# Transposes of values and keys by VectorE in 32x32 blocks, placed by GpSimd, in a bidirectional RWKV-7 and short-convolution step

## The chip, the core and the metric

The kernel runs on one core of a Trainium2 chip. The metric is the device time of one execution in microseconds (us). Five engines work side by side, each through its own instructions in order: PE (TensorE, matmuls; its weight loads are listed apart as PEld), DVE (VectorE), ACT (ScalarE), POOL (GpSimd) and SP (SyncE, which here only issues DMAs).

## What is computed

One layer of a diffusion backbone for 128 context tokens and 256 latent tokens, 2048 channels. After a norm, one projection `h @ w_in` feeds an RWKV-7 time mixing in both directions and a gated short convolution; both go through output projections, are merged by gates and projected again. All is float32. The part that the change touches is the time mixing, whose recurrence for each of 32 heads of 64 channels is

```python
sa = einsum('dbhij,dbhj->dbhi', S, a_t)
S = S * w_t[..., None, :] + sa[..., :, None] * b_t[..., None, :] + v_t[..., :, None] * k_t[..., None, :]
y = einsum('dbhij,dbhj->dbhi', S, r_t)
```

in two directions `d`, from a zero state for the context and from a given state for the latent tokens. `w` is the decay, `k` the key, `v` the value, `a = -kk` and `b = kk * a`.

## The kernel before

**Blocks.** The recurrence is done for 16 blocks of two heads (`b`, 128 channels on the partitions), each in chunks of 64 tokens: six chunks for each direction, twelve in all (`f`). Within a chunk the recurrence becomes matrices. The stages of one block, each a generator:

- `prep_a`, `prep_k`: decay, learning rate and normalised key of the next block, by small matmuls and elementwise work.
- `prep_b` (line 664): `pr` (queries times decay) and `bk` (keys over decay) are multiplied on PE to the decay products `pA` (line 700), twelve matmuls of two passes each for a direction; VectorE masks them into the tile `A` (line 706). A triangular 32x32 system in each half chunk has then to be inverted: its blocks go by DMA through DRAM (`ui`, line 710) into a tile `U` of 48 partitions (line 716), 60 small dependent VectorE instructions solve it in place (lines 721 and 723; called *the solve* below), ScalarE makes the transposed copy `UT` (line 727), and both go back by DMA through DRAM (`uo`, lines 728 and 729) into `A` (line 734) and a tile `x11` (line 735; the profile calls it `x`). GpSimd multiplies `bk` by the chunk's last decay in between (line 713).
- `prep_c` (line 737): PE transposes the values into `pv` (six transposes of 128x128, line 761; ScalarE copies the values reversed in time first, for the second direction, line 758), and ten of the twelve chunks of `bk` into `pb` (line 770); ScalarE copies these out of PSUM into `sav` and `bt` (lines 763 and 771). Then come the products `pav` (line 776), whose result goes behind the values into `sav`, and a GpSimd memset of the lower half of `A` (line 783).
- `scan` (line 794): first the corner products `pH` from `x11` and `A` (line 852) and `pX`; then two chains of chunks, context and latent, each step `po`, `pq`, `pu`, and last `py` (line 893), which reads `sav`.
- `norm` (line 910) and `finish` (line 927): a group norm on VectorE with a power on GpSimd (`rs`, line 924), then three PE transposes of the result (`py` again, line 931).

**What fills PE.** Beside this runs the stream of the large projections (`Stream`): all weights are loaded in raw tiles of 1 MB (two buffers), split by ScalarE and VectorE into a high and a low part (`whi`, line 88, and `wlo`, line 89, three buffers each), and each product is three matmuls (lines 81 to 83, called a *triple* below) into `d_...` tiles. PE's order is written out by hand: every `yield n` of a stage puts `n` triples behind it, `prep_b` yields PB0 = 14 and PB1 = 6 (line 93), and before `scan` the triples are filled up to WINDOW = 80 (line 974; 104 in the first block, 96 in the last). So each steady block has the same number of triples, 160, whatever the yields within `prep_c` are. The other engines' orders, SP's too, are made by a scheduler from dependencies, priorities and its own estimate of times; their instructions wait in that order.

Of the kernel before, what the change touches and what calls it, by code (L numbers as in the profile page):

```python
# [56 lines left out]
def hybrid_step(ctx, tc, cst, x_prompt, x_sample, state_f, state_b, c, c_ctx, ada_w, ada_b, norm_g,  # L57
# [605 lines left out]

    def prep_b(b, o):

        r, kk = r_[b], o["kk"]
# [27 lines left out]
        for d in range(2):  # L694
            pr, bk = o["pr"][d], o["bk"][d]
            m0 = C_MB if d else C_MF
            pas = {(h, n0): bank(f"pA_{b}_{d}_{h}_{n0}") for n0 in (0, 4) for h in range(2)}
            for n in range(NCH):
                for h in range(2):
                    TE.matmul(pas[h, n // 4 * 4][:, n % 4, :], bk[hss[h], n, :], pr[hss[h], n, :],  # L700
                              start=True, stop=True)
            for n0, w in ((0, 4), (4, 2)):
                mk = cs[:, m0:m0 + P].rearrange("p (w t) -> p w t", t=C).unsqueeze(1).broadcast_to([P, w, 2, C])
                for h in range(2):
                    f0 = NCH * d + n0
                    V.tensor_tensor(A[:, :, f0:f0 + w, hss[h]].rearrange("p w n t -> p n w t"),
                                    pas[h, n0][:, 0:w, :].rearrange("p n (w t) -> p n w t", t=C), mk, ALU.mult)
# [4 lines left out]
        for d in range(2):
            G.tensor_tensor(o["bk"][d][:], o["bk"][d][:], o["ep"][d][:, :, C:C + 1].broadcast_to([P, NCH, P]), ALU.mult)
# [13 lines left out]
        S.copy(UT[:], U[:].rearrange("p a b -> p b a"))  # L727
# [8 lines left out]

    def prep_c(b, o):

        r, v, A = r_[b], v_[b], o["A"]
# [10 lines left out]
        sav = sp.tile([P, 2 * NCH, P], F32, tag="sav", name=f"sav_{b}")  # L750
        bt = sp.tile([P, 2 * NCH, P], F32, tag="bt", name=f"bt_{b}")
        o["sav"], o["bkt"] = sav, bt
        for d in range(2):
            if d == 0:
                src = v
            else:
                src = tmp(f"vr_{b}")
                S.copy(src[:], v[:, ::-1])
            pv = bank(f"pv_{b}_{d}")
            for q in range(3):  # L760
                TE.transpose(pv[:, q, :], src[:, q * P:(q + 1) * P], ident)
# [405 lines left out]
```

## Time and profile before

| what | value |
|---|---|
| time, median of 3 runs | 2238.22 us (2237.42 to 2239.56) |
| the profiled execution's own time | 2242.0 us |
| its span, first to last instruction | 2240.2 us |
| PE busy, its weight loads | 97%, 92% |
| DVE, ACT, POOL busy | 69%, 47%, 5% |
| DMA | 339.97 MB, mean 152 GB/s |
| granted TensorE clock | 0.996 |

Busy shares are of the span. In a timeline a row gives the start in us from the span's start, the duration in us, the engine, the line, the operation, out<-in and shapes, and in brackets the idle time before it and what ended it. PE's durations overlap, since matmuls are pipelined: what one costs is read from the distance between starts.

### The profile page before, as it was taken

The numbers are of one execution on the slowest core, as the hardware profiler recorded it, in microseconds if no ns is written. First come the engines' busy times: TensorE is split into PE (matmuls) and PEld (weight loads), VectorE is DVE, ScalarE is ACT, GpSimd is POOL, SyncE is SP. The second block draws the span as 40 slices with busy tenths as digits, with TensorE's granted clock in tenths as the row PEclk, the third lists the DMA queues.
The fourth block names the chain that finished last, engine by engine and source line by source line (L and its number), as shares of the span: only waits on it lengthen the run. The fifth ranks groups of instructions, "written<-read, shape, count | busy, mean of one in ns | idle before, by whom it ended". The sixth has DMA issues, their size and how long they took to land.

```text
span 2240.2 us, 40545 instructions
## 1 busy us (share of the span) xinstructions
PE 2179.2 (97%) x16020; PEld 2064.9 (92%) x16020; DVE 1540.2 (69%) x3208; ACT 1044.3 (47%) x1800; POOL 116.5 (5%) x113
## 2 busy tenths in 40 slices
PE   5899999999999999999999999999999999999998
PEld 3588999999999999999999999999999999998988
DVE  3248567787777778777878787777777774444354
ACT  4245445454545454454545454546455543333333
POOL 2000010101010100000010101010100000000000
PEclk9999999999999999999999999999999999999999
DMA  9973544444444445443444434444445455886633
GB/s 335 346 211 116 147 129 133 111 120 125 112 125 120 113 117 132 115 132 103 124 109 133 111 110 134 112 118 140 120 121 143 146 179 162 292 281 230 221 132 113
DMA packets 440397, 339.97 MB, mean 152 GB/s; under 512 B 95552, under 2 KB 421776, under 8 KB 439312
## 3 DMA queue, kind: packets, MB, share of 16 engines
q1 hardware_dynamic: 438720, 335.63, 51.1%
q8 instruction: 126, 2.06, 0.4%
q10 hardware_dynamic: 432, 1.57, 0.2%
q14 instruction: 63, 0.52, 0.1%
q0 software_dynamic: 1056, 0.19, 0.1%
HBM read 307.37 MB, written 29.36 MB: 150 GB/s over the span
## 4 chain that ended last, share of the span: by engine, by line
PE 81%; DVE 8%; DMA 5%; ACT 3%; SPq 2%; issue 1%; POOL 0%; POOLq 0%; ACTq 0%; DVEq 0%
PE d_rk L81 4%; PE d_rk L83 4%; PE d_rk L82 4%; PE d_gv L81 3%; PE d_gv L82 3%; PE d_gv L83 3%; DMA raw_adah<-in_ada_w_dram 3%; PE pA L700 2%; PE d_oa L81 2%; PE d_oa L83 2%; PE d_oa L82 2%; PE d_bc L81 2%; PE d_mb L81 2%; PE d_bc L83 2%; PE d_bc L82 2%; PE d_bx L81 2%
## 5 line engine op out<-in xcount | busy, mean ns | idle before, releaser
L721 DVE TENSOR_TENSOR ut<-U 48x30 f32<-48x30 f32 (+14 forms) x480 | 154.6, 322 | 16.2 <-DMA U<-ui 4.1
L81 PE MATMUL d_rk<-h_hi,whi_rk 128*128 128x384 f32 x480 | 163.0, 340 | 0.6 <-ACT lst L554 0.6
L723 DVE TENSOR_TENSOR U<-U,ut 48x30 f32<-48x30 f32 (+14 forms) x480 | 154.5, 322 | 12.1
L81 PE MATMUL d_gv<-h_hi,whi_gv 128*128 128x384 f32 x480 | 161.0, 335 | 0.0
L83 PE MATMUL d_gv<-h_hi,wlo_gv 128*128 128x384 f32 x480 | 160.7, 335 | 0.0
L82 PE MATMUL d_gv<-h_lo,whi_gv 128*128 128x384 f32 x480 | 160.7, 335 | 0.0
L83 PE MATMUL d_rk<-h_hi,wlo_rk 128*128 128x384 f32 x480 | 160.4, 334 | 0.0
L82 PE MATMUL d_rk<-h_lo,whi_rk 128*128 128x384 f32 x480 | 160.4, 334 | 0.0
L88 ACT CAST whi_gv<-raw_gv 128x1024 fp32r<-128x1024 f32 (+1 forms) x64 | 64.0, 1000 | 139.6 <-PE d_rk L82 96.9
L88 ACT CAST whi_rk<-raw_rk 128x1024 fp32r<-128x1024 f32 x60 | 63.0, 1054 | 106.4 <-PE d_rk L82 31.7
L89 DVE TENSOR_TENSOR wlo_rk<-raw_rk,whi_rk 128x1024 fp32r<-128x1024 f32 x60 | 72.9, 1218 | 44.9 <-ACT whi_rk L88 39.7
L81 PE MATMUL d_gb<-h_hi,whi_gb 128*128 128x384 f32 x256 | 92.2, 360 | 0.0
L924 POOL TENSOR_TENSOR rs<-var,nhalf 128x6 f32<-128x6 f32 x16 | 21.2, 1325 | 1364.1 <-DVE var L922 1364.1
L81 PE MATMUL d_bc<-h_hi,whi_bc 128*128 128x384 f32 x256 | 92.2, 360 | 0.0
L81 PE MATMUL d_bg<-h_hi,whi_bg 128*128 128x384 f32 x256 | 92.1, 360 | 0.0
L81 PE MATMUL d_bx<-h_hi,whi_bx 128*128 128x384 f32 x256 | 92.1, 360 | 0.0
L81 PEld LDWEIGHTS d_rk<-h_hi,whi_rk 128*128 128x128 f32 x480 | 90.1, 188 | 1.8 <-ACT lst L554 0.9
L81 PE MATMUL d_ma<-h_hi,whi_ma 128*128 128x384 f32 x256 | 91.7, 358 | 0.0
L81 PE MATMUL d_ob<-ybh,whi_ob 128*128 128x384 f32 x256 | 88.9, 347 | 2.6 <-ACT whi_ob L88 2.1
L81 PEld LDWEIGHTS d_gv<-h_hi,whi_gv 128*128 128x128 f32 x480 | 90.5, 189 | 0.2
L82 PEld LDWEIGHTS d_gv<-h_lo,whi_gv 128*128 128x128 f32 x480 | 90.5, 188 | 0.0
L83 PEld LDWEIGHTS d_gv<-h_hi,wlo_gv 128*128 128x128 f32 x480 | 90.4, 188 | 0.0
(315 smaller groups left out, 6641.9 us busy)
## 6 DMA issues: line engine op xcount, KB each, us to landing
raw_adah<-in_ada_w_dram SPq DMA_DIRECT2D x64, 512.0 KB, 8.6
raw_rk<-in_w_in_dram SPq DMA_DIRECT2D x60, 512.0 KB, 5.3
raw_gv<-in_w_in_dram SPq DMA_DIRECT2D x60, 512.0 KB, 4.9
raw_ma<-in_w_in_dram SPq DMA_DIRECT2D x16, 1024.0 KB, 5.5
raw_mb<-in_w_in_dram SPq DMA_DIRECT2D x16, 1024.0 KB, 5.7
raw_bc<-in_w_in_dram SPq DMA_DIRECT2D x16, 1024.0 KB, 5.5
raw_bx<-in_w_in_dram SPq DMA_DIRECT2D x16, 1024.0 KB, 5.4
raw_bg<-in_w_in_dram SPq DMA_DIRECT2D x16, 1024.0 KB, 5.5
```

The lines of the kernel that those rows point to most:

```text
L81: TE.matmul(out, wh, xh, start=start, stop=False)
L82: TE.matmul(out, wh, xl, start=False, stop=False)
L83: TE.matmul(out, wl, xh, start=False, stop=stop)
L88: S.copy(hi[0:rows], src)
L89: V.tensor_tensor(lo[0:rows], src, hi[0:rows].bitcast(F32), ALU.subtract)
L700: TE.matmul(pas[h, n // 4 * 4][:, n % 4, :], bk[hss[h], n, :], pr[hss[h], n, :], start=True, stop=True)
L721: V.tensor_tensor(tv, U[:, 0:s, s:s + 1].broadcast_to([48, s, w]), U[:, s:s + 1, s + 1:].broadcast_to([48, s, w]), ALU.mult)
L723: V.tensor_tensor(U[:, 0:s, s + 1:], U[:, 0:s, s + 1:], tv, ALU.add)
L924: G.tensor_tensor(rs[:], var[:], nhalf[:], ALU.pow)
```

## The change

The sixteen PE transposes of a block go, and with them the PSUM tiles `pv` and `pb`, six `yield 1` of `prep_c` and ten ScalarE copies (one reversed copy of the values, four out of `pv`, four out of `pb`, and that of `UT`). In their place:

- at the start of `prep_b` VectorE transposes the values of a direction in 32x32 blocks into a temporary `vt` (two instructions of 128x384), and GpSimd copies the blocks where they belong in `sav`: 16 copies of 32 partitions x 192 elements;
- behind the last mask of `A`, VectorE transposes `bk` in place in 32x32 blocks (two instructions of 128x768), and GpSimd copies the blocks into `bt`, all twelve chunks: 32 copies of the same size;
- the transposed copy `UT` is GpSimd's.

```diff
     def prep_b(b, o):
-        r, kk = r_[b], o["kk"]
+        r, kk, v = r_[b], o["kk"], v_[b]
+        sav = sp.tile([P, 2 * NCH, P], F32, tag="sav", name=f"sav_{b}")
+        o["sav"] = sav
+        for d in range(2):
+            x = tmp(f"vt_{b}_{d}")
+            V.transpose(x[:], v[:, ::-1] if d else v[:])
+            x = x[:].rearrange("p (n e t) -> p n e t", e=2, t=32)
+            for e in range(2):
+                for q in range(4):
+                    G.tensor_copy(sav[C + 32 * e:C + 32 * e + 32, NCH * d:NCH * d + NCH, 32 * q:32 * q + 32],
+                                  x[32 * q:32 * q + 32, :, e, :])
...
         for d in range(2):
-            G.tensor_tensor(o["bk"][d][:], o["bk"][d][:], o["ep"][d][:, :, C:C + 1].broadcast_to([P, NCH, P]), ALU.mult)
+            o["lam"] = G.tensor_tensor(o["bk"][d][:], o["bk"][d][:], o["ep"][d][:, :, C:C + 1].broadcast_to([P, NCH, P]),
+                                       ALU.mult).ins
+        with tc.issue_after(last):
+            for d in range(2):
+                V.transpose(flat(o["bk"][d][:]), flat(o["bk"][d][:]))
...
-        S.copy(UT[:], U[:].rearrange("p a b -> p b a"))
+        G.tensor_copy(UT[:], U[:].rearrange("p a b -> p b a"))
...
     def prep_c(b, o):
-        for d in range(2):
-            if d == 0:
-                src = v
-            else:
-                src = tmp(f"vr_{b}")
-                S.copy(src[:], v[:, ::-1])
-            pv = bank(f"pv_{b}_{d}")
-            for q in range(3):
-                TE.transpose(pv[:, q, :], src[:, q * P:(q + 1) * P], ident)
-            for e in range(2):
-                S.copy(sav[C:P, NCH * d + e:NCH * d + NCH:2, :], pv[C * e:C * e + C, 0:3, :])
-            yield 1
-        for d in range(2):
-            for n0, n1 in (((0, 4), (4, 5)), ((0, 3), (4, 6)))[d]:
-                pb = bank(f"pb_{b}_{d}_{n0}")
-                for n in range(n0, n1):
-                    TE.transpose(pb[:, n - n0, :], o["bk"][d][:, n, :], ident)
-                S.copy(bt[:, NCH * d + n0:NCH * d + n1, :], pb[:, 0:n1 - n0, :])
-                yield 1
+        with tc.issue_after(o["lam"]):
+            for d, p, q in ((d, p, q) for d in range(2) for p in range(4) for q in range(4)):
+                G.tensor_copy(bt[32 * p:32 * p + 32, NCH * d:NCH * d + NCH, 32 * q:32 * q + 32],
+                              o["bk"][d][32 * q:32 * q + 32, :, 32 * p:32 * p + 32])
```

`last` is the last mask of `A`; `issue_after` holds an instruction's place in the order behind the named one. On PE the six triples that stood between the transposes now stand behind `pav`, before the next matmuls of `prep_a`; nothing else moves there. In three places the other engines' orders are of interest. Line numbers behind the change are those of the changed kernel.

GpSimd, from one block's memset of `A` over the end of that block (power `rs`) to the next block's memset, blocks 3 and 4, before:

```order
L783 MEMSET A_5063 64x1536
L924 TENSOR_TENSOR rs_6146<-var_6143,nhalf 128x6
L713 TENSOR_TENSOR bk_0_6150<-bk_0_6150,ep_1148 128x768
L713 TENSOR_TENSOR bk_1_6156<-bk_1_6156,ep_1150 128x768
L783 MEMSET A_6214 64x1536
```

and with the change (`vt_0` and `vt_1` are the two directions' turned values of block 4, `xN` tells of N such instructions):

```order
L782 MEMSET A_5150 64x1536
L743 COPY UT_5310<-U_5246 48x1024
L676 COPY sav_6237<-vt_0_6238 32x6x32 x7
L923 TENSOR_TENSOR rs_6234<-var_6231,nhalf 128x6
L676 COPY sav_6237<-vt_0_6238 32x6x32
L676 COPY sav_6237<-vt_1_6248 32x6x32 x8
L725 TENSOR_TENSOR bk_0_6259<-bk_0_6259,ep_1148 128x768
L725 TENSOR_TENSOR bk_1_6265<-bk_1_6265,ep_1150 128x768
L770 COPY bt_6503<-bk_0_6259 32x6x32 x16
L770 COPY bt_6503<-bk_1_6265 32x6x32 x16
L782 MEMSET A_6323 64x1536
```

The power `rs` of block 3's norm now stands behind seven copies of block 4's values (in 12 of 15 such places; behind 14 in two and 9 in one), and the memset behind the 32 copies of the keys.

VectorE, the end of the solve of block 4, before (`ut` and `U` are the solve, `wlo_bc_0_1` a low part of the stream's weights, `ga` a gate):

```order
L89 TENSOR_TENSOR wlo_bc_0_0_6692<-raw_bc_0_6689,whi_bc_0_0_6691 128x1024
L721 TENSOR_TENSOR ut_6310<-U_6308 48x108
L723 TENSOR_TENSOR U_6308<-U_6308,ut_6310 48x27x4
L721 TENSOR_TENSOR ut_6310<-U_6308 48x84
L725 TENSOR_SCALAR U_6308<-U_6308 48x32
L723 TENSOR_TENSOR U_6308<-U_6308,ut_6310 48x28x3
L721 TENSOR_TENSOR ut_6310<-U_6308 48x58
L723 TENSOR_TENSOR U_6308<-U_6308,ut_6310 48x29x2
L721 TENSOR_TENSOR ut_6310<-U_6308 48x30
L723 TENSOR_TENSOR U_6308<-U_6308,ut_6310 48x30
L89 TENSOR_TENSOR wlo_bc_0_1_6696<-raw_bc_0_6689,whi_bc_0_1_6695 128x1024
L440 TENSOR_TENSOR ga_6735<-ga_6735,d_gv_0_6628 128x384
```

and with the change:

```order
L741 TENSOR_SCALAR U_6419<-U_6419 48x32
L89 TENSOR_TENSOR wlo_bc_0_1_6806<-raw_bc_0_6799,whi_bc_0_1_6805 128x1024
L739 TENSOR_TENSOR U_6419<-U_6419,ut_6421 48x28x3
L737 TENSOR_TENSOR ut_6421<-U_6419 48x58
L739 TENSOR_TENSOR U_6419<-U_6419,ut_6421 48x29x2
L440 TENSOR_TENSOR ga_6845<-ga_6845,d_gv_0_6738 128x384
L737 TENSOR_TENSOR ut_6421<-U_6419 48x30
L739 TENSOR_TENSOR U_6419<-U_6419,ut_6421 48x30
L89 TENSOR_TENSOR wlo_bc_1_0_6887<-raw_bc_1_6884,whi_bc_1_0_6886 128x1024
```

One `wlo` and one `ga` now stand inside the solve. This is so in the even blocks 2 to 12 (in 4, 8 and 12 another `wlo` has moved out ahead of the solve); in the odd ones from 3 on and in 14 the solve holds the same other instructions as before.

SP, the way back of the inverse in block 4, before:

```order
L101 DMA raw_bc_1_6774<-in_w_in_dram 128x8x256
L728 DMA uo_6213<-U_6308 48x1024
L729 DMA uo_6213<-UT_6372 48x1024
L734 DMA A_6214<-uo_6213 32x12x32 x2
L735 DMA x_4_6376<-uo_6213 32x12x32
L734 DMA A_6214<-uo_6213 32x12x32 x2
L735 DMA x_4_6376<-uo_6213 32x12x32
L101 DMA raw_bx_0_6906<-in_w_in_dram 128x8x256
```

and with the change:

```order
L101 DMA raw_bc_1_6884<-in_w_in_dram 128x8x256
L101 DMA raw_bx_0_7016<-in_w_in_dram 128x8x256
L744 DMA uo_6322<-U_6419 48x1024
L745 DMA uo_6322<-UT_6483 48x1024
L621 DMA lraw_0_8049<-in_w_dram 96x2x128
L750 DMA A_6323<-uo_6322 32x12x32 x2
L751 DMA x_4_6487<-uo_6322 32x12x32
L750 DMA A_6323<-uo_6322 32x12x32 x2
L751 DMA x_4_6487<-uo_6322 32x12x32
L101 DMA raw_bx_1_7172<-in_w_in_dram 128x8x256
```

A load of 1 MB of weights now stands ahead of the inverse's way back, and a small load within it, again in the even blocks 2 to 12. In the odd blocks 3 to 13 and in block 14 a 1 MB load stands between `uo<-UT` and `A<-uo` in both kernels.

More of the change, by code (lines that the diff above doesn't have):

```diff
@@ L705, in prep_b @@
                     f0 = NCH * d + n0
-                    V.tensor_tensor(A[:, :, f0:f0 + w, hss[h]].rearrange("p w n t -> p n w t"),
-                                    pas[h, n0][:, 0:w, :].rearrange("p n (w t) -> p n w t", t=C), mk, ALU.mult)
+                    last = V.tensor_tensor(A[:, :, f0:f0 + w, hss[h]].rearrange("p w n t -> p n w t"),
+                                           pas[h, n0][:, 0:w, :].rearrange("p n (w t) -> p n w t", t=C), mk,
+                                           ALU.mult).ins
             yield PB1
@@ L712, in prep_b @@
         for d in range(2):
-            G.tensor_tensor(o["bk"][d][:], o["bk"][d][:], o["ep"][d][:, :, C:C + 1].broadcast_to([P, NCH, P]), ALU.mult)
+            o["lam"] = G.tensor_tensor(o["bk"][d][:], o["bk"][d][:], o["ep"][d][:, :, C:C + 1].broadcast_to([P, NCH, P]),
+                                       ALU.mult).ins
+        with tc.issue_after(last):
+            for d in range(2):
+                V.transpose(flat(o["bk"][d][:]), flat(o["bk"][d][:]))
         U = sp.tile([48, 32, 32], F32, tag="U", name=f"U_{b}")
@@ L737, in prep_c @@
     def prep_c(b, o):
-        r, v, A = r_[b], v_[b], o["A"]
+        r, A, sav = r_[b], o["A"], o["sav"]
         s_in = sp.tile([P, 2, C], F32, tag="s_in", name=f"s_in_{b}")
@@ L748, in prep_c @@
                                       [:, :, 32 * jb:32 * jb + 32])
-        sav = sp.tile([P, 2 * NCH, P], F32, tag="sav", name=f"sav_{b}")
         bt = sp.tile([P, 2 * NCH, P], F32, tag="bt", name=f"bt_{b}")
-        o["sav"], o["bkt"] = sav, bt
-        for d in range(2):
-            if d == 0:
-                src = v
-            else:
-                src = tmp(f"vr_{b}")
-                S.copy(src[:], v[:, ::-1])
-            pv = bank(f"pv_{b}_{d}")
-            for q in range(3):
-                TE.transpose(pv[:, q, :], src[:, q * P:(q + 1) * P], ident)
-            for e in range(2):
-                S.copy(sav[C:P, NCH * d + e:NCH * d + NCH:2, :], pv[C * e:C * e + C, 0:3, :])
-            yield 1
-        for d in range(2):
-            for n0, n1 in (((0, 4), (4, 5)), ((0, 3), (4, 6)))[d]:
-                pb = bank(f"pb_{b}_{d}_{n0}")
-                for n in range(n0, n1):
-                    TE.transpose(pb[:, n - n0, :], o["bk"][d][:, n, :], ident)
-                S.copy(bt[:, NCH * d + n0:NCH * d + n1, :], pb[:, 0:n1 - n0, :])
-                yield 1
+        o["bkt"] = bt
+        with tc.issue_after(o["lam"]):
+            for d, p, q in ((d, p, q) for d in range(2) for p in range(4) for q in range(4)):
+                G.tensor_copy(bt[32 * p:32 * p + 32, NCH * d:NCH * d + NCH, 32 * q:32 * q + 32],
+                              o["bk"][d][32 * q:32 * q + 32, :, 32 * p:32 * p + 32])
         pvs = [bank(f"pav_{b}_{d}") for d in range(2)]
```

## The prediction

> **What bounds the kernel now.** First the page, its span and the engines' shares; then for whom PE waited (us in total, times, longest).
>
> ```profile
> span 2240.2 us, 40545 instructions
> PE 2179.2 (97%) x16020; PEld 2064.9 (92%) x16020; DVE 1540.2 (69%) x3208; ACT 1044.3 (47%) x1800; POOL 116.5 (5%) x113
> ```
>
> ```profile
> PE pada L292 <- DMA raw_adah<-in_ada_w_dram: 22.9, 14, 10.1
> ...
> PE pH L852 <- DMA x<-uo: 0.2, 1, 0.2
> ...
> PE py L931 <- DVE ytok L925: 0.2, 1, 0.2
> ```
>
> PE is busy nearly throughout, and behind the start (`pada`) it waits for almost nobody. What PE no longer does is won, as long as nobody else becomes late. The two waits of 0.2 us tell where that is near: at `pH`, whose operand comes back by DMA from the solve, and at the last `py`, which needs the norm. So I looked at two blocks in the timeline. Block 4 (628 to 733 us): the loads of `x11` with first and last start and time to landing, and the start of `pH`.
>
> ```profile
> L735 SPq DMA_DIRECT2D x<-uo x2: 303/385/467, 679.6 to 681.0; - x2
> ...
> DMA to landing us min/median/max: 1.8/1.9/2.0
> ```
>
> ```profile
> 686.17 0.62 PE L852 MATMUL pH<-x,A 32*32 32x32 f32 x48
> ```
>
> The second load lands at 681.0 + 2.0 = 683.0 at the latest, 3.2 us ahead of `pH`. Block 5 (733 to 838 us), where a 1 MB load of weights stands on SP just ahead of these loads:
>
> ```profile
> L735 SPq DMA_DIRECT2D x<-uo x2: 450/754/1057, 784.8 to 787.2; - x2
> ...
> DMA to landing us min/median/max: 3.7/4.5/5.4
> ```
>
> ```profile
> 791.31 0.62 PE L852 MATMUL pH<-x,A 32*32 32x32 f32 x48
> ```
>
> Here they land at 784.8 + 5.4 = 790.2 and 787.2 + 3.7 = 790.9, 0.4 us ahead of `pH`. What makes this chain long is the solve. VectorE's costliest groups during block 5's solve (749.4 to 778.7 us):
>
> ```profile
> L723 DVE TENSOR_TENSOR U<-U,ut 48x30 f32<-48x30 f32 (+14 forms) x30 | 9.7, 323 | 0.8
> L721 DVE TENSOR_TENSOR ut<-U 48x30 f32<-48x30 f32 (+14 forms) x30 | 9.7, 322 | 1.0 <-DMA U<-ui 0.3
> L89 DVE TENSOR_TENSOR wlo_gv<-raw_gv,whi_gv 128x1024 fp32r<-128x1024 f32 x4 | 4.9, 1213 | 0.0
> ```
>
> VectorE idles 1.8 us in 29: whatever is added to it there, or holds it up there, ends the solve later.
>
> **PE's part.** Block 5's transposes, from the last triple ahead of them to `pav`:
>
> ```profile
> 742.48 0.34 PE L83 MATMUL d_bg<-h_hi,wlo_bg 128*128 128x384 f32 x1
> 742.65 0.49 PE L761 MATMUL pv<-cs,v 128*128 128x128 f32 x3
> 742.89 0.42 PE L81 MATMUL d_bg<-h_hi,whi_bg 128*128 128x384 f32 x1
> 743.15 0.34 PE L82 MATMUL d_bg<-h_lo,whi_bg 128*128 128x384 f32 x1
> ...
> 747.38 0.34 PE L83 MATMUL d_rk<-h_hi,wlo_rk 128*128 128x384 f32 x1
> 747.65 1.61 PE L776 MATMUL pav<-sav,A 64*64 64x64 f32 x48
> ```
>
> Three transposes take 0.24 us, and the first matmul behind them 0.26 where others take 0.17. From 742.65 to 747.65 are 5.00 us. Six triples, at 18 x 0.173, are 3.12 of them, and 0.10 is the step to `pav` (0.27 for 0.17), which stays. That leaves 1.78 us a block, **28.5 us** in 16 blocks. All of it lies between `pA` and `pH`, so PE comes to `pH` 1.78 us earlier against a chain that starts at `pA` as before: at 684.4 in block 4, at 789.5 in block 5. Ten ScalarE copies go too; with ScalarE busy 47% and off this path they count nothing.
>
> **VectorE's part.** Two group rows:
>
> ```profile
> L673 DVE TENSOR_TENSOR bk<-kd,sig 128x384 f32<-128x384 f32 x32 | 17.6, 551 | 0.1
> ...
> L792 DVE STREAM_TRANSPOSE st<-s_in 64x64 f32<-64x64 f32 x64 | 12.2, 221 | 0.6
> ```
>
> A block transpose of 64 columns takes 0.22 us, and a column by the slope of the products 1.04 ns ((1213 - 551) / 640): 0.55 us for each `vt`, 0.48 from start to start, and 0.95 for each `bk`. Those of `bk` stand between the masks and the solve:
>
> ```profile
> 739.07 1.95 DVE L706 TENSOR_TENSOR A<-pA,cs 128x512 f32<-128x512 f32 x4 [0.63 <-PE pA L700]
> ...
> 747.01 0.56 DVE L480 TENSOR_TENSOR bu<-bu,d_bg 128x384 f32<-128x384 f32 x1 [2.75 <-PE d_bg L83]
> ...
> 749.44 0.18 DVE L721 TENSOR_TENSOR ut<-U 48x30 f32<-48x30 f32 x1 [0.28 <-DMA U<-ui]
> ```
>
> There VectorE idles for 2.75 us in one go, and the solve waits for its DMA, so their 1.9 us are hidden; without that cover they would count whole. Within the solve, blocks 2, 6 and 10 get a `wlo` (1.13 to the next start) and a `ga` (0.47) more, 1.6 us; blocks 4, 8 and 12 net a `ga`, 0.5.
>
> **GpSimd's part.** The trace has no copy on GpSimd. The nearest rows, GpSimd's own and ScalarE's copy of `UT`:
>
> ```profile
> L713 POOL TENSOR_TENSOR bk<-bk,ep 128x768 f32<-128x768 f32 x32 | 50.2, 1568 | 157.1 <-PE pA L700 145.7 <-issue 4.6 <-DMA raw_rk<-in_w_in_dram 3.4
> ...
> L584 POOL MEMSET ep<- 128x390 f32 x4 | 1.5, 425 | 0.0
> ...
> L579 POOL MEMSET st<- 128x256 f32 x2 | 0.6, 309 | 37.5 <-PE pe L83 37.5
> ```
>
> ```profile
> L727 ACT COPY UT<-U 48x1024 f32<-48x1024 f32 x16 | 33.8, 2112 | 34.1 <-DVE U L723 34.1
> ```
>
> By the memsets a column costs 0.87 ns and an instruction 0.09 us; by the product of two inputs, less that 0.09, a column costs 1.93 ns. A copy of 192 columns then takes 0.25 to 0.46 us; I take 0.35, since it reads one tensor, more than a memset and less than a product. `UT`'s 1024 columns take 0.98 to 2.06 us; I take 1.5, which is 0.6 less than on ScalarE. [...]
>
> Do the copies hold up VectorE? Twice in this trace GpSimd's product meets VectorE instructions with two SBUF inputs:
>
> ```profile
> 306.28 0.55 DVE L934 TENSOR_TENSOR ya<-ya,bon 128x384 f32<-128x384 f32 x1
> 306.73 1.49 POOL L713 TENSOR_TENSOR bk<-bk,ep 128x768 f32<-128x768 f32 x1 [5.21 <-PE pA L700]
> ...
> 307.35 1.27 DVE L935 TENSOR_TENSOR ya<-ya,ga 128x384 f32<-128x384 f32 x1
> ```
>
> ```profile
> 194.04 1.21 DVE L89 TENSOR_TENSOR wlo_mb<-raw_mb,whi_mb 128x1024 fp32r<-128x1024 f32 x1
> 194.22 2.37 POOL L713 TENSOR_TENSOR bk<-bk,ep 128x768 f32<-128x768 f32 x1 [4.65 <-issue]
> ```
>
> The second `ya` takes 1.27 instead of 0.55 and ends 0.40 behind the product; in the other place the product takes 2.37 instead of 1.49 and waits `wlo` out. They exclude each other. [...]
>
> The solve consists of such instructions. The 32 key copies start at 742.0 (masks end at 741.0, then one `bk`) and last 11 us or more, the solve starts at 749.4: 12 to 20 copies meet it. Their delay `c` lies between 0 (nothing excluded) and 7 us (20 x 0.35 waited out whole); I take 2, nearer to 0, because between two dependent instructions the port is free for a while: `ya` needed it for 0.40 of its 0.55. `UT` starts behind the `wlo` that now follows the solve, 1.1 us, and is 0.6 shorter: `u` = 0.5.
>
> **SP's part.** In the even blocks the small load ahead of `A<-uo` costs an issue, 0.5 as with `x`; the 1 MB load ahead of `uo<-U` costs up to the difference of the landings above, 4.5 - 1.9 = 2.6, of which I take 1.5, since it starts earlier. In block 5's kind that load waited for a `wlo` that PE paces:
>
> ```profile
> 781.82 1.22 DVE L89 TENSOR_TENSOR wlo_gb<-raw_gb,whi_gb 128x1024 fp32r<-128x1024 f32 x1 [3.11 <-ACT whi_gb L88]
> ```
>
> With PE it comes up to 1.78 earlier; I take 1.5 off.
>
> **The sum.** Block 5's kind (seven blocks: 3 to 13 odd, and 14): `x11` lands at 790.9 - 1.5 + 2.5 = 791.9, PE waits 2.4. Block 4's (4, 8, 12): 683.0 + 0.5 + 2.0 + 2.5 = 688.0, PE waits 3.6; with 1.6 for 0.5 (2, 6, 10) 4.7. 16.8 + 10.8 + 14.1 = **41.7 us**. Blocks 0, 1 and 15 are filled differently; I count no wait there.
>
> The norm has seven value copies ahead of `rs` now. VectorE and GpSimd at the end of block 4, then that of block 3 with PE's `py`:
>
> ```profile
> 729.56 0.55 DVE L921 TENSOR_REDUCE var<-ysq 128x6 f32<-128x384 f32 x1
> 730.14 0.17 DVE L922 TENSOR_SCALAR var<-var 128x6 f32<-128x6 f32 x1
> ```
>
> ```profile
> 625.43 0.56 DVE L925 TENSOR_TENSOR ytok<-ytok,rs 128x384 f32<-128x384 f32 x1 [1.50 <-POOL rs L924]
> ```
>
> ```profile
> 627.77 0.49 PE L931 MATMUL py<-cs,ytok 128*128 128x128 f32 x3
> ```
>
> The slack is 627.77 - 625.99 = 1.8 us here, and about 0 where PE waited; I take it as even between 0.2 and 1.8. The copies start when `vt_0` ends, 1.25 us ahead of the end of `var` (0.48, then the two rows above), and the `vt` themselves delay `var` by about 0.45 (0.96, half of it hidden by ScalarE's square). So `rs` is late by 7 x 0.35 - 1.25 + 0.45 = 1.65 us, and PE waits 0.66 on average. Twelve such, two with 14 copies (4.1 late, 3.1 waited), one with nine (1.35): **15 us**.
>
> Altogether -28.5 + 41.7 + 15 = +28.2 on the profiled execution's 2242.0, which is 3.8 above the median of the runs: 2266.4, say **2266 us**.
>
> **Rivals.** One more row, GpSimd's memset in block 5, which runs beside the start of the solve:
>
> ```profile
> 749.39 1.38 POOL L783 MEMSET A<- 64x1536 f32 x1 [8.24 <-PE pav L776]
> ```
>
> (1) *The cover holds*, faster: copies take 0.25 us and exclude nobody, `UT` is 1.1 us shorter and waits for no `wlo`. Then `x11` lands at 788.3 and at 684.1 at most, ahead of PE in all blocks, and the norm costs 6 us (0.95 late): -22.5, 2216 us. For it: that memset held up nothing, the solve's rows above show no idle time. Against: the two rows of exclusion, and the 0.4 us of slack in seven blocks. It decides below `c` + `u` = 0.1. (2) *GpSimd shuts VectorE out*: queued without a wait between, the copies keep the port until 742.0 + 11.2 = 753.2; VectorE then has some 3.5 us of work ahead of the solve, which starts at 757 instead of 749.4: `c` = 7.4, waits of 7.8, 9.0 and 10.1, 112 us in all, +98, 2336 us. For it: nothing separates 16 copies but GpSimd's own issue. Against: in the second place above GpSimd got the port as soon as `wlo` was through. (3) *The terms cancel*: `c` near 0.5 and 0.25 us a copy, within 4.5 us of before. That transposes stay on PE is excluded, its order holds none.
>
> **How the numbers follow.** About 0.2%, 4.5 us, is what a measurement of this kernel can tell from no change. Forecast 0.48 (own range 2240 to 2306, by `c` + `u` from 0.7 to 5.2), rival 1 0.28, rival 2 0.12, rival 3 0.12: faster 0.28, same 0.12, slower 0.60. The range takes in rival 1 and leaves out most of rival 2: 2214 to 2325.
>
> **What would show it.** Right: among PE's waits `pH` for `x` with some 40 us and `py` for `ytok` with some 15; idle time or longer means in the solve's rows; GpSimd's copies between 0.25 and 0.46 us; no rows of `pv` and `pb`. Wrong: `pH` waiting under 10 us in total, or a new wait of PE at `pav`, `pq` or `pu` for GpSimd.

## The result and the profile after

The changed kernel takes 2297.9 us (median of 4 runs, 2293.8 to 2299.1), the kernel before 2238.3: a ratio of 1.0259, 95% interval 1.0246 to 1.0272, or 59.6 us more. The forecast was 2266, 28 more: the right side, and less than half the size. The profiled execution took 2296.9 us, 54.9 more than that of before. The first page of its profile, span and engines:

```profile
span 2295.1 us, 40734 instructions
## 1 busy us (share of the span) xinstructions
PE 2177.9 (95%) x15764; PEld 2056.4 (90%) x15764; DVE 1634.4 (71%) x3272; ACT 956.1 (42%) x1640; POOL 532.6 (23%) x897
```

PE has 256 instructions fewer and is busy for just as long. So look at two places: for whom it waits, and how fast it runs. PE's waits (us in total, times, longest):

```profile
PE pH L851 <- DMA x<-uo: 20.6, 21, 1.8
PE py L930 <- DVE ytok L924: 17.5, 12, 5.5
PE pl L83 <- DVE lwl L89: 17.1, 15, 1.9
...
PE pav L775 <- DVE A L717: 3.1, 3, 2.4
```

Of before, `pH` and `py` stood at 0.2 each, and `pl`, a small product of the next block's `prep_a` ahead of `pH`, at 1.7. So these three cost 53.1 us more. Now the granted clock, of before and of after:

```profile
core 0: 2240.2 us, clock 0.996
```

```profile
core 0: 2295.1 us, clock 0.987
```

The time that the clock did not grant, (1 - clock) x span, was 8.0 us and is 30.6 (with the clocks not rounded, 0.9964 and 0.9867). A part of that falls on time in which PE waits anyway; on busy PE it was 4.9 us and is 25.4, some 21 us more. Where it goes shows in PE's timeline at the start of block 5, behind the longest wait for the norm, with the granted clock by stretches (the column behind the engines' busy times) under it:

```profile
746.60 0.87 PE L930 MATMUL py<-cs,ytok 128*128 128x128 f32 x3 [5.48 <-DVE ytok L924]
747.40 2.93 PE L711 MATMUL pA<-pr,bk 64*128 64x128 f32 x24
...
751.39 0.52 PE L81 MATMUL d_bg<-h_hi,whi_bg 128*128 128x384 f32 x1
751.71 0.52 PE L82 MATMUL d_bg<-h_lo,whi_bg 128*128 128x384 f32 x1
...
752.80 0.34 PE L83 MATMUL d_bg<-h_hi,wlo_bg 128*128 128x384 f32 x1
752.98 0.33 PE L81 MATMUL d_bg<-h_hi,whi_bg 128*128 128x384 f32 x1
```

```profile
744.00:747.00 3.00, 0.40 (x2) 0.43 (x3) 0.56 (x1) 0.00 (x0) 2.77 (x5) 0.79 0.57 141
747.00:750.00 3.00, 3.00 (x27) 2.67 (x25) 1.79 (x4) 1.07 (x2) 0.04 (x1) 0.50 0.03 5
750.00:753.00 3.00, 3.00 (x14) 2.78 (x13) 2.14 (x5) 1.04 (x1) 1.48 (x1) 0.57 0.36 90
753.00:756.00 3.00, 3.00 (x34) 2.75 (x32) 0.83 (x2) 0.00 (x0) 0.00 (x0) 1.00 0.18 28
```

Behind the wait the matmuls of the stream start 0.32 us apart, then 0.17 again: for a while the clock was half. In the records of the clock such stretches are 3.41 us long, or twice that; a full one loses 1.7 us of work. Before there were three while PE was busy, two of them in the prologue; after there are fourteen, eleven of them behind the prologue. In the 3.41 us ahead of each of the eleven PE had been busy for 0.00 to 2.20 us.

The ledger of the profiled executions: -28.5 for the transposes (as counted; see the account of the prediction below), +20.4 `pH`, +15.4 `pl`, +17.3 `py`, about +21 half clock, +6.7 other waits (`pav`, `pA` and the products of the last weights, mostly in the last block), together 52.3 of 54.9. The rest was not traced; a part of it is that PE starts slowly behind a wait: 0.28 us from `pl` to the next start behind each of its waits past the prologue, for 0.17 without one.

### The profile page after: what moved, and what is told of

It is laid out like the page before. It is cut to its first block, busy times and chain, and to the rows that moved or that the text cites. A ratio compares the mean times of both kernels' runs of the same rounds, so it can differ in the third digit from the quotient of the medians.

```text
span 2295.1 us, 40734 instructions
## 1 busy us (share of the span) xinstructions
PE 2177.9 (95%) x15764; PEld 2056.4 (90%) x15764; DVE 1634.4 (71%) x3272; ACT 956.1 (42%) x1640; POOL 532.6 (23%) x897
## 4 chain that ended last, share of the span: by engine, by line
PE 50%; DVE 29%; DMA 8%; issue 4%; ACT 3%; POOL 3%; SPq 2%; DVEq 0%; POOLq 0%; ACTq 0%
DVE ut L737 5%; DVE U L739 5%; DMA raw_adah<-in_ada_w_dram 3%; DVE wlo_gv L89 3%; PE pA L711 2%; PE d_oa L81 2%; PE d_oa L83 2%; PE d_oa L82 2%; DMA x<-uo 2%; PE d_mb L81 2%; PE d_gb L81 1%; PE d_mb L83 1%; PE d_mb L82 1%; PE acc L82 1%; PE acc L83 1%
## 5 line engine op out<-in xcount | busy, mean ns | idle before, releaser
L676 POOL COPY sav<-vt 32x192 f32<-32x192 f32 x256 | 123.1, 481 | 825.1 <-ACT ysq L918 473.2
L770 POOL COPY bt<-bk 32x192 f32<-32x192 f32 x512 | 236.2, 461 | 34.0 <-DVE bk L729 13.0
L737 DVE TENSOR_TENSOR ut<-U 48x30 f32<-48x30 f32 (+14 forms) x480 | 167.0, 348 | 15.3 <-DMA U<-ui 3.3
L739 DVE TENSOR_TENSOR U<-U,ut 48x30 f32<-48x30 f32 (+14 forms) x480 | 164.8, 343 | 11.8
L743 POOL COPY UT<-U 48x1024 f32<-48x1024 f32 x16 | 47.4, 2964 | 352.5 <-DVE U L739 327.7
```

The lines of the kernel that those rows point to most:

```text
L676: G.tensor_copy(sav[C + 32 * e:C + 32 * e + 32, NCH * d:NCH * d + NCH, 32 * q:32 * q + 32], x[32 * q:32 * q + 32, :, e, :])
L737: V.tensor_tensor(tv, U[:, 0:s, s:s + 1].broadcast_to([48, s, w]), U[:, s:s + 1, s + 1:].broadcast_to([48, s, w]), ALU.mult)
L739: V.tensor_tensor(U[:, 0:s, s + 1:], U[:, 0:s, s + 1:], tv, ALU.add)
L743: G.tensor_copy(UT[:], U[:].rearrange("p a b -> p b a"))
L770: G.tensor_copy(bt[32 * p:32 * p + 32, NCH * d:NCH * d + NCH, 32 * q:32 * q + 32], o["bk"][d][32 * q:32 * q + 32, :, 32 * p:32 * p + 32])
```

## The experiments

Expectations speak of Theory A, formed from the trace above: each of the added waits delays PE by itself, and waits of some length are followed by half clock. Its rivals are in each text. Measured (median in us; ratio to the kernel before with its 95% interval; then, of one profiled execution, PE's waits at `pl` and `pH` together, at `py` and at `pav`, a dash where its list has none, and the clock):

| kernel | time | ratio | pl+pH | py | pav | clock |
|---|---|---|---|---|---|---|
| before | 2238.3 | 1 | 1.9 | 0.2 | - | 0.996 |
| changed | 2297.9 | 1.0259 (1.0246 to 1.0272) | 37.7 | 17.5 | 3.1 | 0.987 |
| ut_scalar | 2287.7 | 1.0219 (1.0204 to 1.0234) | 24.1 | 17.4 | 2.4 | 0.987 |
| rs_first | 2291.3 | 1.0238 (1.0218 to 1.0259) | 42.7 | 3.3 | 7.7 | 0.983 |
| window84 | 2289.1 | 1.0225 (1.0205 to 1.0244) | 30.5 | 15.2 | - | 0.989 |
| b_window72 | 2242.5 | 1.0014 (1.0005 to 1.0024) | 8.0 | - | - | 0.995 |
| keys_pe | 2279.0 | 1.0180 (1.0165 to 1.0195) | 14.3 | 17.0 | 0.2 | 0.991 |
| values_pe | 2278.9 | 1.0176 (1.0161 to 1.0191) | 24.1 | 0.2 | 7.6 | 0.990 |
| bt_scalar | 2322.5 | 1.0374 (1.0357 to 1.0392) | 46.2 | 17.7 | 2.7 | 0.980 |
| b_ut_late | 2302.2 | 1.0283 (1.0268 to 1.0299) | 33.7 | 0.2 | - | 0.985 |
| val_late | 2268.8 | 1.0133 (1.0118 to 1.0149) | 4.2 | 3.3 | 17.6 | 0.990 |
| all_late | 2274.0 | 1.0162 (1.0145 to 1.0179) | 5.2 | 3.2 | 23.0 | 0.987 |
| val_late7 | 2244.7 | 1.0026 (1.0016 to 1.0036) | 6.3 | 3.2 | - | 0.994 |
| all_late13 | 2241.7 | 1.0016 (1.0007 to 1.0024) | 16.1 | 3.3 | - | 0.994 |
| all_late_pe15 | 2235.2 | 0.9982 (0.9973 to 0.9991) | 12.1 | 3.3 | 0.5 | 0.997 |
| all_late_pe15_h | 2239.5 | 1.0001 (0.9992 to 1.0009) | 11.2 | 2.3 | 0.5 | 0.997 |
| b_h | 2257.9 | 1.0082 (1.0069 to 1.0096) | 5.7 | 2.0 | - | 0.997 |

**Does a wait halve the clock? b_ut_late.** The kernel before, with nothing new on GpSimd or VectorE:

```diff
-        S.copy(UT[:], U[:].rearrange("p a b -> p b a"))
+        for _ in range(3):
+            S.copy(UT[:], U[:].rearrange("p a b -> p b a"))
```

> The kernel before with the transposed copy UT made three times over on ScalarE, so that x11 lands 4.2 us later; GpSimd and VectorE do nothing new. PE then waits at pl (whose high part stands behind UT on ScalarE) or at pH, 4.2 us less the slack: 3.8 us in seven blocks, 1 to 2.5 us in six, 37 to 45 us together. Theory A (a wait of PE over about 1.5 us within a 3.41 us window is followed by a window of half clock, 1.7 us lost): 8 windows more or above, clock about 0.99, time 2239 + 40 + 14 = about 2293 us. Rival D (half clock comes from the added work of GpSimd or VectorE): clock 0.996, time about 2279 us.

Measured 2302.2, 64 us more. The engines, PE's waits and the clock of this kernel:

```profile
PE 2209.2 (96%) x16020; PEld 2084.6 (90%) x16020; DVE 1540.9 (67%) x3208; ACT 1107.0 (48%) x1832; POOL 115.6 (5%) x113
```

```profile
PE pl L81 <- ACT lwh L88: 21.4, 13, 2.1
...
PE pl L83 <- DVE lwl L89: 10.9, 14, 1.7
```

```profile
core 0: 2304.3 us, clock 0.985
```

GpSimd is busy 5% as before, yet the clock is lower than in the changed kernel, and PE's same 16020 instructions take 30 us longer. Waits of 33.7 us (31.8 more) cost 64: twice their length. Half clock on busy PE took 30.3 us here for 4.9 before, 25.4 of the 64. Theory A's 2293 was 9 too low, and Rival D (2279, clock 0.996) is out. Only ScalarE has more work here (1107.0 us for 1044.3); that this is not what lowers the clock is told by all_late and all_late13 below, where ScalarE is busy for 988.9 and 987.6 us at clocks of 0.987 and 0.994. The wait of block 4 is short: its first part took 1.96 us, its second 0.65, and the stretches by 3 us show the clock go.

```profile
687.00:690.00 3.00, 1.31 (x8) 0.99 (x6) 1.85 (x4) 2.97 (x7) 0.00 (x0) 1.00 0.51 98
690.00:693.00 3.00, 2.07 (x7) 1.75 (x8) 2.35 (x6) 2.69 (x5) 0.00 (x0) 0.63 0.42 66
693.00:696.00 3.00, 3.00 (x11) 3.00 (x11) 0.36 (x1) 0.58 (x1) 0.00 (x0) 0.50 0.41 115
```

PE was busy for 1.31 of 3 us, not idle throughout, and that was enough. In the 3.41 us ahead of each of the thirteen half stretches behind the prologue PE was busy for 1.15 to 2.02 us. So waits of about 2 us were enough here, with PE idle for about half of such a stretch.

**Two that did not intervene as meant: window84 and b_window72.** One number is changed, in window84 in the changed kernel, in b_window72 (to 72) in the kernel before:

```diff
-    PRO, WINDOW, FIRST, LAST = 32, 80, 24, 16
+    PRO, WINDOW, FIRST, LAST = 32, 84, 24, 16
```

> The changed kernel with four more triples ahead of each pH (WINDOW 84 for 80), so that PE comes to pH 2.1 us later and the same triples are missing at the end of the stream. Theory A (PE's waits set the half-clock windows): pH falls from 20.6 us to under 3 us, about six windows of half clock near pH go (10 us); pl and py stay: time about 2268 us. Rival D (half clock comes from GpSimd's or VectorE's added work, not from PE's waits): the windows stay at 13 or more, time about 2278 us.

> The kernel before, with eight triples fewer ahead of each pH (WINDOW 72 for 80): PE comes to pH 4.2 us earlier, x11 lands as before, GpSimd and VectorE do nothing new. From the slacks of the kernel before PE waits some 3.8 us in seven blocks and 1 to 2.5 us in six: about 37 us at pH. Theory A (a wait of PE over about 1.5 us within one 3.41 us window is followed by a window of half clock that loses 1.7 us): 7 to 10 such windows more, clock about 0.99, time 2238 + 37 + 14 = about 2289 us. Rival D (half clock comes from the added work on the other engines): no such window more, time about 2275 us.

The second changed only the first blocks and the last: in the steady ones the triples ahead of `pH` are set by the loop that waits for the stream's `gv` products, not by WINDOW, and `pH` starts 58.0 us behind `pA` as before. So its 2242.5 says nothing on Theory A. The first moved the stream against the blocks, so that each block met other loads; `pH` fell to 4.3, `pl` rose to 26.2. Its 2289.1 is neither Theory A's 2268 nor Rival D's 2278. It shows only that a wait at one of the two turns into a wait at the other.

**UT on ScalarE: ut_scalar.** The changed kernel with one instruction moved back:

```diff
-        G.tensor_copy(UT[:], U[:].rearrange("p a b -> p b a"))
+        S.copy(UT[:], U[:].rearrange("p a b -> p b a"))
```

> The changed kernel with the transposed copy UT on ScalarE again. Theory A (formed from the trace after): GpSimd's UT waits 0.9 us for a VectorE instruction, then shuts VectorE out for its 2.1 us (wlo_gb behind the solve took 2.66 us instead of 1.21), so the low part lwl is late and PE waits at pl: 17.1 us in all. With UT on ScalarE pl waits under 4 us, UT takes 2.1 us, and pl and pH together wait about 0.9 x 15 = 13.5 us less than their 37.7. PE idles less, so fewer windows of half clock, each worth 1.7 us: time about 2278 us (2270 to 2284). Rival B (pl waits because the whole solve ends later, the UT copy shuts nobody out): pl keeps over 10 us, wlo behind the solve stays long, time within 5 us of 2298.

First what GpSimd's `UT` did in the changed kernel, block 5: GpSimd's row, then VectorE's from the solve's last instruction on.

```profile
797.01 3.02 POOL L743 COPY UT<-U 48x1024 f32<-48x1024 f32 x1 [21.48 <-DVE U L739]
```

```profile
796.73 0.21 DVE L739 TENSOR_TENSOR U<-U,ut 48x30 f32<-48x30 f32 x1
796.86 1.21 DVE L89 TENSOR_TENSOR wlo_gb<-raw_gb,whi_gb 128x1024 fp32r<-128x1024 f32 x1
797.99 0.54 DVE L440 TENSOR_TENSOR ga<-ga,d_gv 128x384 f32<-128x384 f32 x1
798.45 2.66 DVE L89 TENSOR_TENSOR wlo_gb<-raw_gb,whi_gb 128x1024 fp32r<-128x1024 f32 x1
```

`UT` waits the first `wlo_gb` out (to 798.07) and then works for 2 us; `ga`, which reads one SBUF tensor and one in PSUM, runs beside it in its usual 0.54; the next `wlo_gb`, with two SBUF inputs, takes 2.66 us for 1.21 and ends 1.08 us behind `UT`. So this copy with a single input kept a `wlo` out until it was done, and was itself kept out by one for 1.06 us. That much of Theory A held: with `UT` on ScalarE the mixing of `v` (L422) is back from a mean of 752 ns to 412. But `pl` did not go under 4 us, as Theory A had it. `pH` fell from 20.6 to 0.9 us, and `pl` rose from 17.1 to 23.2; more than half of that is a wait for another:

```profile
PE pl L81 <- ACT lwh L88: 13.3, 6, 2.6
PE pl L83 <- DVE lwl L89: 9.9, 15, 1.6
```

`UT` now stands ahead of `lwh` in ScalarE's queue, and the solve ends as late as in the changed kernel (48.7 us behind the block's first `pA` in both, 46.1 in the kernel before; means of blocks 3 to 14). `pl` and `pH` together fell by 13.6 us, as expected; the clock stayed at 0.987, so the time fell by 10 and not by 20, between Theory A and Rival B.

**The power ahead of the copies: rs_first.** The copies of the values are held behind the previous block's `rs`:

```diff
+        with tc.issue_after(box["rs"]):
             for e in range(2):
                 for q in range(4):
                     G.tensor_copy(sav[...], x[...])
...
-        G.tensor_tensor(rs[:], var[:], nhalf[:], ALU.pow)
+        box["rs"] = G.tensor_tensor(rs[:], var[:], nhalf[:], ALU.pow).ins
```

> The changed kernel with the sixteen value copies of a block held behind the power rs of the block before. Theory A (the norm's power stands in GpSimd's queue behind the copies): py falls from 17.5 us to under 3 us, and with the two longest waits (5.5 us each) four windows of half clock go (6.8 us): time about 2276 us (2270 to 2281). Rival C (the work is only pushed on: the keys' products, turns and copies come later, the solve starts later): py falls as well, but pH and pl grow by what it falls: within 5 us of 2298.

In the changed kernel, end of block 4, GpSimd's rows and VectorE's:

```profile
738.10 6.36 POOL L676 COPY sav<-vt 32x192 f32<-32x192 f32 x14 [50.55 <-DVE vt L672]
744.54 1.32 POOL L923 TENSOR_TENSOR rs<-var,nhalf 128x6 f32<-128x6 f32 x1
```

```profile
740.28 0.32 DVE L921 TENSOR_SCALAR var<-var 128x6 f32<-128x6 f32 x1
...
745.89 0.56 DVE L924 TENSOR_TENSOR ytok<-ytok,rs 128x384 f32<-128x384 f32 x1 [5.02 <-POOL rs L923]
```

`var` is there at 740.6, `rs` starts at 744.5. With `rs` first `py` fell from 17.5 to 3.3, so the queue was its cause; but `pl` and `pH` rose to 42.7 and `pav` to 7.7: 6.6 us gained of 14. The profiled execution was the slowest of four (2298.6 us); its clock of 0.983 was 0.985 to 0.986 in the others, no better than the changed kernel's 0.985 to 0.987. Rival C was largely right, with 2291.3 for its "within 5 of 2298": the work was pushed on, and the solve ends 49.3 us behind `pA` for 48.7.

**The halves: keys_pe, values_pe, bt_scalar.** Each takes a part of the change back (shortened here). keys_pe and values_pe put the code of the kernel before in the place of VectorE's turns and GpSimd's copies, bt_scalar moves the 32 copies of the keys:

```diff
 keys_pe
-                V.transpose(flat(o["bk"][d][:]), flat(o["bk"][d][:]))
-                G.tensor_copy(bt[...], o["bk"][d][...])
+                    TE.transpose(pb[:, n - n0, :], o["bk"][d][:, n, :], ident)
+                S.copy(bt[:, NCH * d + n0:NCH * d + n1, :], pb[:, 0:n1 - n0, :])
+                yield 1
 values_pe
-            V.transpose(x[:], v[:, ::-1] if d else v[:])
-                    G.tensor_copy(sav[...], x[...])
+                TE.transpose(pv[:, q, :], src[:, q * P:(q + 1) * P], ident)
+                S.copy(sav[C:P, NCH * d + e:NCH * d + NCH:2, :], pv[C * e:C * e + C, 0:3, :])
+            yield 1
 bt_scalar
-                G.tensor_copy(bt[...], o["bk"][d][...])
+                S.copy(bt[...], o["bk"][d][...])
```

> The values half of the change alone (with UT on GpSimd): the keys are transposed on PE and copied by ScalarE as before, no copies of keys on GpSimd. PE saves six transposes a block, 0.66 us, 10.6 us in all. Theory A (the copies of keys beside the solve cost it 0.12 to 0.19 us an instruction, 1.1 to 1.5 us a solve; the copies of values cost at py): the solve's rows are back at 322 ns, pl and pH together wait about 10 us (37.7 in the changed kernel), py keeps about 17, half clock falls to some 12 us lost: 2239 - 11 + 17 + 10 + 8 = about 2263 us. Rival F (the solve ends late for the wlo and ga that now stand inside it and for UT's copy, the copies of keys do little): pl and pH keep 25 us or more, about 2280 us.

> The keys half of the change alone (with UT on GpSimd): the values are transposed on PE as before, no copies of values ahead of the power rs. PE saves ten transposes a block, 1.12 us, 17.9 us in all. Theory A: py falls to 0.2 us, the solve's rows stay near 345 ns, pl and pH together wait 35.8 - 16 x 0.66 = about 25 us more than before, half clock loses some 10 us more: 2239 - 18 + 25 + 10 = about 2256 us. Rival G (the waits for the norm bring most of the half clock): the clock is back at 0.995, about 2246 us.

> The changed kernel with the 32 copies of the keys of a block on ScalarE in place of GpSimd, all else the same (VectorE turns the blocks). Theory A (GpSimd's copies and the solve's instructions exclude each other; ScalarE's do not): the solve's rows fall from 343 and 348 ns to 322, each solve ends 1.1 to 1.5 us earlier, pl and pH together fall from 37.7 to about 18 us, half clock by some 5 us: about 2273 us. Rival H (it is reading the same tensors, or ScalarE's 32 copies of about 0.3 us hold up the casts that PE waits for): the solve's rows stay over 340 ns, or PE waits for whi: 2290 us or more.

The solve's rows of the changed kernel, then of keys_pe (VectorE, last numbers: busy, mean ns of one, idle):

```profile
L737 DVE TENSOR_TENSOR ut<-U 48x30 f32<-48x30 f32 (+14 forms) x480 | 167.0, 348 | 15.3 <-DMA U<-ui 3.3
L739 DVE TENSOR_TENSOR U<-U,ut 48x30 f32<-48x30 f32 (+14 forms) x480 | 164.8, 343 | 11.8
```

```profile
L733 DVE TENSOR_TENSOR ut<-U 48x30 f32<-48x30 f32 (+14 forms) x480 | 154.7, 322 | 67.9 <-DMA U<-ui 55.6
L735 DVE TENSOR_TENSOR U<-U,ut 48x30 f32<-48x30 f32 (+14 forms) x480 | 154.4, 322 | 11.1
```

Without GpSimd's copies beside it the solve is at its 322 ns, in bt_scalar too, where the same copies read the same tensors from ScalarE. So (26 + 21) x 30 = 1.4 us a solve is the price of the exclusion; the odd blocks, where the solve holds the same instructions as before, show it directly, with 30.7 us from the solve's start to its end for 29.3. Either half alone loses 41 us, and the two add up to more than the whole's 60: `UT` on GpSimd, worth 10 us by ut_scalar, is in both. keys_pe, at `pl` and `pH` 14.3, lies between Theory A's 10 and Rival F's 25, and its 2279.0 us are Rival F's 2280 and not Theory A's 2263: its solve still ends 47.4 us behind `pA` for 46.1 before. values_pe missed both its times, 2256 and 2246, by 23 us and more. There `py` is gone and the clock is 0.990, not 0.995, so Rival G is out; its 7.6 us at `pav` come from the code of the experiment, which puts the values' transposes directly ahead of `pav`. bt_scalar is the slowest of all: the solve's instructions are short, yet the solve ends later (50.8 us behind `pA` for 48.7), and PE waits 46.2 us at `pl` and `pH`. Rival H's time of 2290 or more came, though not for `whi`: most of the wait is for `lwl`. Moving work off the contended engine onto another that PE also depends on was worse; which of ScalarE's instructions came late was not followed up.

**The whole without its waits: val_late, all_late and their seconds.** The copies of the values stand behind `lam` (so behind `rs`), `UT` is ScalarE's; all_late has the whole change, with the copies of the keys held behind the solve by a copy of one column that reads `U`; val_late has the values' half.

```diff
+        with tc.issue_after(o["lam"]):
+            for d, e, q in ((d, e, q) for d in range(2) for e in range(2) for q in range(4)):
+                G.tensor_copy(sav[...], vt[d][...])
...
-        with tc.issue_after(o["lam"]):
+        with tc.issue_after(G.tensor_copy(dm[:], o["U"][:, 0, 31:32]).ins):
             for d, p, q in ...:
                 G.tensor_copy(bt[...], o["bk"][d][...])
+        yield 8
         pvs = [bank(f"pav_{b}_{d}") for d in range(2)]
...
-        yield 2
```

> The values half alone with its found costs taken out: GpSimd's copies of the values stand behind the products of the keys with the last decay (behind rs and lam, not ahead of them), three triples stand between the last transpose of the keys and pav to cover them, UT is on ScalarE, the keys are transposed on PE. Theory A: PE saves 10.6 us, py waits 3 us at most, the solve's rows are at 322 ns, pl and pH together wait 5 us, half clock stays near the 5 us lost in the kernel before: about 2234 us (2228 to 2245). Rival F (the wlo and ga inside the solve of the even blocks and SP's order cost by themselves): pl and pH keep 12 us with half clock behind them, 2250 us or more.

> The whole change with its found costs taken out: copies of the values behind lam, eight triples ahead of pav to cover them, UT on ScalarE, and the copies of the keys held behind the end of the solve by a one-column copy that reads U. Theory A: 28.5 us of PE saved, py 3 us, the solve's rows at 322 ns, but PE comes 1.78 us earlier to pl and pH against a solve that ends as before: 1.4 us in seven blocks and about 0.5 in six, 13 us, with some 8 us of half clock and restarts: about 2235 us (2222 to 2255). Rival F (wlo and ga inside the solve, and the copies beside the low parts behind the solve, cost as much again): 2262 us or more.

Both theories missed the place: `pl`, `pH` and `py` nearly went, and the wait moved to `pav`, for the copies that now come later (17.6 and 23.0 us), with half clock behind it; the times, 2268.8 and 2274.0, missed Theory A's by 35 and 39 us. So the next two give `pav` more triples ahead, `yield 7` for 3 and `yield 13` for 8:

> The kernel val_late with seven triples in place of three ahead of pav, 2.1 us later, so that the copies of the values (0.49 us each beside the masks and the solve) are done. Theory A (each wait of PE costs itself, some 0.15 us of restart and, over about 1.5 us within a window, half clock): pav falls from 17.6 us to under 3, the half clock behind it goes (12 us): 2269 - 15 - 9 = about 2245 us or below. Rival F (the wait only moves to pl or pH, since the chain from pA to pH is as long as PE's work): within 8 us of 2269.

> The kernel all_late with thirteen triples in place of eight ahead of pav, 2.6 us later. Theory A: pav falls from 23.0 us to under 3, and half clock from 26.8 us to under 10: 2274 - 20 - 17 = about 2237 us, as low as 2225 if the restarts go too. Rival F (the wait moves to pl or pH, which stand at 2.6 us each): within 8 us of 2274.

Some 2 us more of triples ahead of each `pav` brought 24 and 32 us, near Theory A's 2245 and 2237. The waits of 17.6 and 23.0 us at `pav` went, 2.1 and 10.9 us came at `pl` and `pH`, and half clock on busy PE fell from 17.5 to 9.9 and from 26.8 to 9.3 us; the clock rose to 0.994 in both. GpSimd still makes all its copies, 475.6 us of work in all_late13, beside a clock that is nearly that of before. This is the other half of the proof begun with b_ut_late: half clock came with the waits and left with them.

**The last block: all_late_pe15, all_late_pe15_h, b_h.** The first `pA` of block 15, before and in all_late13:

```profile
1784.12 0.38 PE L700 MATMUL pA<-pr,bk 64*128 64x128 f32 x2
```

```profile
1777.05 0.49 PE L708 MATMUL pA<-pr,bk 64*128 64x128 f32 x4
```

So all_late13 has gained 7.1 us up to there, and its span ends 1.4 us later all the same. all_late_pe15 leaves block 15 on PE, by the code of the kernel before; the other two are all_late_pe15 and the kernel before with fewer triples behind `pH`, the first `po` and `pX`:

```diff
-    PB0, PB1, H0, H1, CH0, CH1 = 14, 6, 3, 4, 2, 4
+    PB0, PB1, H0, H1, CH0, CH1 = 14, 6, 2, 2, 2, 4
```

> The kernel all_late13 with the last block's values and keys transposed on PE as before (the sixteen transposes of block 15 alone). Theory A: behind the start of block 15 all_late13 takes 464.5 us where the kernel before takes 456.1, since VectorE's turns and the splits of the last weights meet there; with PE's transposes back the 8.4 go, but for 1: 2241.7 - 7 = about 2235 us (2231 to 2239). Rival J (the last block loses for another reason, the stream's end): within 3 us of 2241.7.

> The kernel all_late_pe15 with the triples behind pH, the first po and pX cut from 3, 3, 4 to 2, 2, 2, so that four more stand ahead of pl and pH (PE comes there 2.1 us later). Theory A: pl and pH fall from 16 us to under 5, with half clock by some 3 us: about 2224 us (2217 to 2232). Rival K (the steps behind pH then come too fast for their copies on ScalarE and VectorE: new waits at po, pq or pX): no gain on all_late_pe15.

> The kernel before with the same cut of the triples behind pH (2, 2, 2). Theory A: it has only some 2 us of waits at pl and pH to lose: 2236 to 2240 us. Rival K: waits at po, pq or pX: 2245 us or more.

all_late_pe15 is the one version that beats both kernels: 2235.2, ratio 0.9982 (0.9973 to 0.9991), 4.5 us under the kernel before beside it (2239.7), as small a gain as these runs can tell. Theory A's 2235 came, and Rival J is out; the traces agree on the reason: block 15's solve starts 34.8 us behind its first `pA` in all_late13 and 27.1 in all_late_pe15, as before (27.0). Its waits and its clock:

```profile
PE pl L83 <- DVE lwl L89: 11.1, 13, 1.7
...
PE py L954 <- DVE ytok L948: 3.3, 3, 1.5
```

```profile
core 0: 2233.6 us, clock 0.997
```

Moving four triples ahead of `pH` made new waits at `pq`, 8.2 us and more, in both kernels: Rival K's outcome. The profile names nobody that `pq` waited for, so Rival K's reason, late copies, is not shown. all_late_pe15_h missed Theory A's 2224 by 15 us. On the kernel before the same cut costs 18 us, so its triples stood well where they were.

Why does PE still wait for `lwl` in all_late_pe15? Block 4 of the kernel before, then of all_late_pe15, with the first `pA` at 628.19 and at 622.52:

```profile
681.36 0.41 DVE L89 TENSOR_TENSOR lwl<-lraw,lwh 96x256 fp32r<-96x256 f32 x1
682.90 0.34 PE L83 MATMUL pl<-l_hi,lwl 96*128 96x384 f32 x1
```

```profile
675.67 0.56 DVE L89 TENSOR_TENSOR lwl<-lraw,lwh 96x256 fp32r<-96x256 f32 x1
676.28 0.45 PE L83 MATMUL pl<-l_hi,lwl 96*128 96x384 f32 x1 [0.71 <-DVE lwl L89]
```

`lwl` ends 53.6 us behind `pA` before and 53.7 here (means of blocks 3 to 14: 53.9 and 53.8), so it is not late. PE, without the transposes, comes 1.8 us earlier to a place where it had 1.1 us to spare: `pl` takes back a part of what the transposes gave.

## Why the prediction was half right

**PE's saving: right.** The first `pA` of block 5 in the kernel before, whose `pav` starts at 747.65; then block 6 of the changed kernel, its first `pA`, and from the end of the triples on to `pav`:

```profile
733.01 0.49 PE L700 MATMUL pA<-pr,bk 64*128 64x128 f32 x4
```

```profile
857.65 0.60 PE L711 MATMUL pA<-pr,bk 64*128 64x128 f32 x6
...
867.13 0.34 PE L83 MATMUL d_bx<-h_hi,wlo_bx 128*128 128x384 f32 x1
867.40 1.09 PE L775 MATMUL pav<-sav,A 64*64 64x64 f32 x30
```

The step is 0.27 as counted. From `pA` to `pav` are 14.64 us with 18 triples before and 9.75 with 12 now; less the 3.12 of six triples, 1.77 us a block went, for 1.78 forecast. Not all of it shows in the whole: in all_late_pe15, at the clock of before and with 15 such blocks (26.7 us), PE is busy for 2157.0 us, 22.2 less. One reason is that PE starts slowly behind a wait, as in the changed kernel: 0.28 us from `pl` to the next start behind a wait (689.60 to 689.88 in block 4), for 0.17. The rest was not followed. VectorE's turns took 0.55 and 0.95 us, as forecast.

**The solve's chain: right in kind, 41.7 forecast, 35.8 measured.** Forecast was the wait at `pH` alone; 15.4 of it came at `pl`, which is ahead of `pH` and depends on VectorE's and ScalarE's work behind the same solve. The prediction gave `pl` no term, though PE's 1.78 us alone use up the 1.1 us to spare there. By blocks, the odd ones from 3 on and 14 waited 16.5 us for 16.8 forecast, the even ones 2 to 12 18.7 for 24.9; which term was too large there, the load on SP or the `wlo`, no run separates. That the total came near is in part luck. The terms: `c` was 1.4 for 2, `u` came out as 0.9 for 0.5, since `UT` takes 3.02 us here and 2.1 where no `wlo` is in its way (2.09 the shortest), the upper bound from the product and not the 1.5 taken. That a copy, which reads one tensor, takes part in the exclusion was the author's estimate, since the rows of before show it for the product alone; `wlo_gb`, at 2.66 us for 1.21 beside `UT`, bears it out. The prediction's "port" is a picture for this: the rows show who waited and for how long, not what the two engines share.

**The norm: right, 15 forecast, 17.3 measured.** A copy alone takes 0.34 us, as taken (0.35), and 0.48 in the mean of the values' copies.

**The step that failed: the sum.** It charged each wait of PE with its own length ("PE waits 2.4") and set that against PE's work at a clock that stays as it is. A sum of 41.7 + 15 = 57 us of waits was on paper, and the row that would have warned, the clock of 0.996 with its few half stretches, was not used. Half clock, at nothing in the sum, took some 21 us more; in b_ut_late waits and half clock together cost twice the waits. With those 21 us the forecast would have been 2287.

**The last block: left out.** "Blocks 0, 1 and 15 are filled differently; I count no wait there." The other waits of 6.7 us lie mostly in block 15, and in all_late13 its turns and copies alone cost 6.5 (2241.7 to 2235.2).

**The rivals.** Rival 1 (the cover holds) fell by the solve's rows, Rival 2 (VectorE shut out for all of the copies) by the same: copies and solve alternate, a solve instruction takes 0.03 to 0.19 us longer beside them, and the solve 1.4 us, where Rival 2 wanted 7.4. Rival 1's 684.1 does not come out of its own terms, which give 684.4 and, in blocks 2, 6 and 10, 685.5. But what Rival 2 foresaw happened at `UT`, where one long copy kept a VectorE instruction out until it ended (`wlo_gb` in block 5, 2.66 us for 1.21). What would show the forecast wrong included "a new wait of PE at `pav`, `pq` or `pu` for GpSimd"; it came at `pl`, for VectorE.
